# Two-layer trunk on one core: other reading orders behind five kinds of head groups, and a later start for the scaling of x's first block

## The chip, the cores and the metric

The kernel runs on 1 core of one Trainium2 chip. The metric is device time in microseconds (us) of one launch. Before the change it is 1683.47 us, the median of 3 runs (1681.31 to 1684.75).

## What is computed

With DEPTH = 1 only the attention layer runs: an RMSNorm, one wide projection into q, k, v and a gate, stick-breaking attention in 32 heads, the SiLU gate, an output projection, the residual and a last RMSNorm. x is 256 rows of 4096, all in float32.

```
def attn_branch(xn, w_in, w_out):
    proj = xn @ w_in                       # (256 x 4096) @ (4096 x 16384)
    q, k, v, g = jnp.split(proj, 4, axis=-1)   # then 32 heads of 128
...
    z = q k^T * scale; log_fail = where(s < t, log_sigmoid(-z), 0)
    a = where(s < t, exp(log_sigmoid(z) + suffix_sum(log_fail)), 0);  o = a @ v
    return (o * jax.nn.silu(g)) @ w_out    # (256 x 4096) @ (4096 x 4096)
h = x + attn_branch(rms_norm(x, norm_attn), w_in, w_out);  return rms_norm(h, final_norm)
```

## The kernel before, in words

**The products.** Both projections are cut into units of 2 x 256 columns from each of two places of the weights (16 units, 0 to 15, for the first projection, 4 for the second), and each unit into 16 steps (0 to 15) over the inner dimension, 256 deep each. Unit 0 is multiplied plainly, 8 products a step; from unit 1 on, a Strassen-like scheme takes 7 products in some steps (`SEVEN`) and 8 in the others. A step's weights come in two tiles, which are cut into parts; parts are numbered n through the whole program, and in unit 0 step s has parts 2s and 2s+1. A float32 product is made of three float32r matmuls (`mm3`): with x = sh + sl and w = wh + wl, a "high" and a "low" half each, TensorE adds up sh\*wh, sh\*wl and sl\*wh in one bank of PSUM. In each of the three the half of x is the stationary operand (128 x 128) and the half of w is the moving one (128 x 512). ScalarE (ACT) makes the highs by casting, VectorE (DVE) the lows by subtraction.

**The order of reading.** The 512 moving columns and the 512 columns of the result are not gone through from left to right. `RUNS` gives two orders: "e" goes through them in runs of 8 (as 4 x 16 x 8) and "c" in runs of 4 (as 4 x 32 x 4); the result is the same. A word of three letters gives the orders of a product's three matmuls. Most products have the word "eee"; the first of each step has "ecc" (`IN_STEP`).

**The heads' groups.** The heads of unit u are worked on while the products of unit u+1 run. For each of a unit's two heads (i = 0, 1) TensorE is given four small groups of other matmuls between two products: `turn` (four transposes of q and k), `scores` (q times k), `scan` (the suffix sums, and a transpose of the gate) and `values` (weights times v, and a transpose). They go in ahead of all waiting products. The function `ten` records such a group, and sets the words of the next seven products: `BEHIND_OTHERS`, which is ("ccc", "ecc", "eee", "eee", "eee", "eee", "ecc"). Where the next group comes sooner than seven products, it sets the list anew. A table `BEHIND`, empty before, could put other words at the head of the list for a group by its name.

**What sets the order of the work.** The class `Plan` is a planner that runs while the program is built: each piece of work has an engine, a cost in ns and a key (its due time), and each engine's next instruction is the waiting one with the smallest key at the planned time. The chip then works through each engine's list strictly in that order; a wait that the planner did not foresee holds up all that stands behind it on the engine.

**The first steps.** `blocks_of(0)` takes x's first block. DVE makes its high and low half at once. The tail of it, reached when these are recorded, is for unit 1: ACT scales the block by the norm's gain in place (`scaled`, two instructions on 128 x 256, written xs<-xs,gcol), and `sums_of` then takes a difference on DVE (128 x 256) and its halves (sh on ACT, sl on DVE, 128 x 256 each). Its key is that of step 2 (`BLOCKS_LATER`), but the work is free to go as soon as an engine has nothing more urgent that is ready. Later blocks of x (xs1, xs2, ...) are loaded by SyncE (SP), scaled and cast on ACT and summed on DVE (four 128 x 128). Their unit 0 halves carry the names sh and sl with the block's number: sl4 is the low half for step 4.

Of the kernel before, what the change touches and what calls it, by code (L numbers as in the profile page):

```python
# [19 lines left out]
P = 128  # L20
# [7 lines left out]
NB = D // CW  # L28
# [6 lines left out]
RUNS = {"e": (4, 8), "c": (4, 4), "g": (2, 8)}  # L35
BEHIND_OTHERS = ("ccc", "ecc", "eee", "eee", "eee", "eee", "ecc")
IN_STEP = ("ecc", "ecc")
BEHIND = {}
WARM, WARM_SHORT, IDLE = 10, 5, 640


# [70 lines left out]
def tensor_ns(n):  # L112
    return 0.4167 * n + 8.5 if n > 128 else 109.0
# [138 lines left out]
def kernel(  # L252
# [10 lines left out]
    nc = Plan(tc)  # L263
# [14 lines left out]
    def minus(out_, full, part):  # L278
        nc.vector.tensor_tensor(out=out_, in0=full, in1=part.bitcast(F32), op=ALU.subtract)
# [49 lines left out]
    def soon(c=4.0):  # L329
        return nc.here + 1e3 * c  # L330
# [13 lines left out]
    FULL_P, FULL_S = (P,) * 2, (W,) * 2  # L344

    since_others, words = 0, BEHIND_OTHERS

    def ten(emit, *n, what):
        def others():
            nonlocal since_others, words  # L350
            first_ = BEHIND.get(what, ())
            since_others, words = 0, first_ + BEHIND_OTHERS[len(first_) :]
            emit()

        return nc.work("tensor", 40 + sum(tensor_ns(m) for m in n), others, nc.here - 1e4, wait=400)
# [209 lines left out]
    def blocks_of(i):  # L565

        key = place_of[0, i]
        tag = ("one", "two", "s", "s")[i % 4]
        yield nc.take(tag)
        pool, inside, bufs = (wp, "s", SINGLES) if tag == "s" else (ap, tag, 1)  # L570
        y = pool.tile([P, KT, S], F32, tag=inside, name=f"xs{i}", bufs=bufs)
        y4 = y.rearrange("p k (a b) -> p (k a) b", a=NT)
        h, l = new_forms(i, "s")
        gain = lambda c: gcol[:, i * KT + c : i * KT + c + 1]
        if i:
            yield moved(
                "sync", lambda: nc.sync.dma_start(y, xT[i]), [KT * S], key - 1, hold=True, wait=1300 * i - 600 if i < 4 else 0
            )

            def scaled():  # L580
                for c in range(KT):
                    nc.scalar.activation(y[:, c, :], y[:, c, :], AF.Copy, scale=gain(c))
                nc.scalar.copy(h[:, 0:4, :], y4)

            yield act(scaled, (S, S, 2 * S), key - 2e3)
            yield dve(lambda: minus(l[:, 0:4, :], y4, h[:, 0:4, :]), 2 * S, key)
        else:
            yield moved("scalar", lambda: nc.scalar.dma_start(gcol, gain_in), [KC], key - 1)
            yield moved("scalar", lambda: nc.scalar.dma_start(y, xT[i]), [KT * S], key - 1, hold=True)
            for c in range(KT):  # L590
                hc, lc = (t[:, 2 * c : 2 * c + 2, :].rearrange("p a b -> p (a b)") for t in (h, l))

                yield dve(
                    lambda: nc.vector.tensor_scalar(out=hc, in0=y[:, c, :], scalar1=gain(c), scalar2=None, op0=ALU.mult),
                    S, key - 1,
                )
                nc.tell(("sh", c))
                yield nc.until(("low", 0, c))
                yield dve(
                    lambda: nc.vector.scalar_tensor_tensor(  # L600
                        out=lc, in0=y[:, c, :], scalar=gain(c), in1=hc.bitcast(F32), op0=ALU.mult, op1=ALU.subtract
                    ),
                    S, key - 1,
                )
        nc.tell(("form", "s", i))
        later = place_at(0, i + BLOCKS_LATER)
        if not i:

            def scaled():
                for c in range(KT):  # L610
                    nc.scalar.activation(y[:, c, :], y[:, c, :], AF.Copy, scale=gain(c))

            yield act(scaled, (S, S), later)
        yield from sums_of(i, y4, "n", later)
        nc.give(tag)
# [214 lines left out]
    BW = 3 * P  # L830
    not_before = off.broadcast_to([P, 2, P])

    def head(u, i):
        act_ = lambda *w: act(*w, soon(4.0 if u else HEADS_FIRST))
        yield nc.take("att", "gh", sooner=True)
        tr = att.tile([P, 2, S], F32, tag="att", name=f"tr{u}_{i}")

        def turn():
            for k in range(2):
                for t in range(NT):  # L840
                    c = k * CW + i * P
                    nc.tensor.transpose(tr[:, k, t * P : (t + 1) * P], st["qk", u][:, t, c : c + P], ident)

        yield ten(turn, P, P, P, P, what=("turn", i))
        if i == HG - 1:
            nc.give("one")
        qk = wp.tile([P, 2, S], F32, tag="gh", name=f"qkT{u}_{i}", bufs=ROWS)
        yield act_(lambda: nc.scalar.copy(qk, tr), 2 * S)
        nc.give("att")
        yield nc.take("att", sooner=True)  # L850
        bank = att.tile([P, W], F32, tag="att", name=f"z{u}_{i}")
        z, gT = bank[:, 0:BW], bank[:, BW:W]

        def turned(to, t):
            nc.tensor.transpose(to, st["gv", u][:, t, i * P : (i + 1) * P], ident)

        def scores():
            kw = dict(stop=False, skip_group_check=True)
            nc.tensor.matmul(z[:, 0:P], qk[:, 1, P:S], qk[:, 0, P:S], start=True, **kw)
            nc.tensor.matmul(z[:, P:BW], qk[:, 1, 0:P], qk[:, 0, :], start=False, **kw)  # L860
            diagonal = z[:, 0 : 2 * P].rearrange("p (a b) -> p a b", a=2)
            nc.tensor.matmul(diagonal, ident_b, not_before, start=False, **kw)

        yield ten(scores, *FULL_P, *FULL_S, 2 * P, what=("scores", i))
        nc.give("gh")
        yield nc.take("gh", sooner=True)

        f = wp.tile([P, BW], F32, tag="gh", name=f"f{u}_{i}", bufs=ROWS)

        def soft():  # L870
            nc.scalar.activation(f, z, AF.Softplus, scale=scale)
            nc.scalar.activation(f, f, AF.Copy, scale=1.0 / scale)

        yield act_(soft, (BW + TABLE, BW))
        yield nc.take("gh", "gh", sooner=True)
        fh, fl = (wp.tile([P, BW], F32R, tag="gh", name=f"f{k}{u}_{i}", bufs=ROWS) for k in "hl")
        yield act_(lambda: nc.scalar.copy(fh, f), BW)
        yield dve(lambda: minus(fl, f, fh), BW)
        nc.give("gh")

        if i == 0:
            yield nc.until(("gate", u))

        def scan():
            kw = dict(start=False, skip_group_check=True)
            nc.tensor.matmul(z, neg_tri, fh, stop=False, **kw)
            nc.tensor.matmul(z, neg_tri, fl, stop=False, **kw)
            nc.tensor.matmul(z[:, 2 * P : BW], neg_one, fh[:, 0:P], stop=False, **kw)
            nc.tensor.matmul(z[:, 2 * P : BW], neg_one, fl[:, 0:P], stop=True, **kw)
            turned(gT, 0)  # L890

        yield ten(scan, BW, BW, P, P, P, what=("scan", i))
        nc.give("gh", "gh")
        gated = st["gv", u][:, :, i * P : (i + 1) * P]
        yield nc.take("gh", sooner=True)
        a = wp.tile([P, BW], F32, tag="gh", name=f"a{u}_{i}", bufs=ROWS)


        def weights_of():
            nc.scalar.activation(a, z, AF.Relu, scale=-scale)  # L900
            nc.scalar.activation(a, a, AF.Exp, scale=-1.0)

        yield act_(weights_of, (BW, BW + TABLE))
        yield act_(lambda: nc.scalar.copy(gated[:, 0, :], gT), P)
        nc.give("att")
        yield nc.take("att", sooner=True)
        bank2 = att.tile([P, BW], F32, tag="att", name=f"o{u}_{i}")
        o, gT2 = bank2[:, 0:S], bank2[:, S:BW]
        v = lambda t: st["gv", u][:, t, CW + i * P : CW + (i + 1) * P]

        def out_of_head():
            kw = dict(skip_group_check=True)
            nc.tensor.matmul(o, v(0), a[:, P:BW], start=True, stop=False, **kw)
            nc.tensor.matmul(o[:, P:S], v(1), a[:, 0:P], start=False, stop=True, **kw)
            turned(gT2, 1)

        yield ten(out_of_head, *FULL_P, *FULL_S, P, what=("values", i))
        nc.give("gh")
        yield act_(lambda: nc.scalar.copy(gated[:, 1, :], gT2), P)
        o2 = o.rearrange("p (t b) -> p t b", t=NT)  # L920
        yield dve(lambda: nc.vector.tensor_tensor(out=gated, in0=o2, in1=gated, op=ALU.mult), S)
        nc.give("att")
# [444 lines left out]
```

## Time and profile before

| | |
|---|---|
| three runs | 1681.31, 1683.47, 1684.75 us |
| the profiled execution | 1683.75 us, span 1681.7 us |
| TensorE (PE) busy | 1666.9 us (99%), 7736 matmuls |
| weight loads (PEld) | 1410.1 us (84%) |
| VectorE (DVE) busy | 1611.1 us (96%) |
| ScalarE (ACT) busy | 1265.1 us (75%) |
| granted TensorE clock | 0.997 over the span |

The span goes from the first to the last instruction; 2.05 us of the profiled execution lie outside it. Matmuls are pipelined: each is shown as busy for about 0.38 us, but the next one starts 0.22 us after it. So what counts in a timeline is the distance from one start to the next, called the pitch here. In a profile's rows acc is a product's bank, tr, z and o are tiles of the heads' groups, wh and wl a part's halves, sh and sl the halves of x. All of TensorE's instructions have one source line, that of a helper, so rows are found by names and times.

### The profile page before, as it was taken

Reading aid. Unit: us, or ns where it says so; the run is one execution under the profiler, and the core shown is the slowest. Engines: PE = TensorE matmul, PEld = TensorE weight load, DVE = VectorE, ACT = ScalarE, POOL = GpSimd, SP = SyncE. Lnnn points to the kernel's source line nnn. Section 1 sums busy time; section 2 is a strip of 40 time slices with the busy share of each in tenths; the row PEclk is TensorE's granted clock in tenths of the full one; section 3 lists DMA queues with packets and bytes.
Section 4 is the critical chain, followed back from the end, with each engine's and each line's share of the span. In section 5 each row is a group of like instructions: output and inputs, shape, how many; then the busy total and the mean of one; then the engine's idle time right before and its main releaser. Section 6 shows DMA issues by size and latency. Waiting matters only on the chain.

```text
span 1681.7 us, 25051 instructions
## 1 busy us (share of the span) xinstructions
PE 1666.9 (99%) x7736; PEld 1410.1 (84%) x7736; DVE 1611.1 (96%) x1851; ACT 1265.1 (75%) x1665; POOL 366.0 (22%) x448
## 2 busy tenths in 40 slices
PE   9999999999999999999999999999999999999997
PEld 7888888888888888888888888888888888888885
DVE  9899999999999999999999999999999978999997
ACT  8896868686868696968686868686878766665664
POOL 0022222222222222222222221222222112212110
PEclk9999999999999999999999999999999999999998
DMA  9978898989897989797989897979898978888895
GB/s 340 350 187 255 228 253 226 263 221 261 225 265 212 271 209 279 199 282 200 278 204 279 216 265 214 260 225 255 229 249 233 290 252 251 268 251 269 254 313 189
DMA packets 254325, 419.31 MB, mean 249 GB/s; under 512 B 28912, under 2 KB 77296, under 8 KB 254192
## 3 DMA queue, kind: packets, MB, share of 16 engines
q1 hardware_dynamic: 195696, 356.34, 63.8%
q0 software_dynamic: 58208, 61.11, 21.8%
q8 instruction: 60, 0.98, 0.3%
q14 instruction: 73, 0.60, 0.1%
q10 hardware_dynamic: 288, 0.28, 0.1%
HBM read 408.17 MB, written 9.44 MB: 248 GB/s over the span
## 4 chain that ended last, share of the span: by engine, by line
PE 98%; DVE 1%; DMA 0%; ACT 0%; issue 0%; SPq 0%; DVEq 0%; ACTq 0%
PE acc L135 93%; PE z L135 3%; PE o L135 1%; PE tr L135 1%; DMA raw<-in_w_in_dram 0%; DVE wl L135 0%; DVE h L135 0%; ACT xs L135 0%; DVE xs L135 0%; SPq L135 0%; ACT sq L135 0%; ACT wh L135 0%; DVE wh L135 0%; DVE scalars L135 0%; ACT scalars L135 0%
## 5 line engine op out<-in xcount | busy, mean ns | idle before, releaser
L135 ACT CAST wh<-raw 128x1024 fp32r<-128x1024 f32 (+1 forms) x1019 | 935.8, 965 | 315.4 <-PE acc L135 131.3
L135 DVE TENSOR_TENSOR wl<-raw,wh 128x1024 fp32r<-128x1024 f32 (+1 forms) x830 | 991.6, 1221 | 35.5 <-PE acc L135 12.7
L135 PE MATMUL acc<-wh,sh 128*128 128x512 f32 x2048 | 767.1, 388 | 0.0
L135 PE MATMUL acc<-wh,sl 128*128 128x512 f32 x1883 | 721.7, 383 | 0.0
L135 PE MATMUL acc<-wl,sh 128*128 128x512 f32 x1718 | 655.1, 381 | 1.1 <-DVE wl L135 1.1
L135 POOL DMA_DIRECT2D raw<-in_w_in_dram x330 | 284.0, 942 | 1000.9 <-DMA raw<-in_w_in_dram 333.0
L135 PEld LDWEIGHTS acc<-wh,sh 128*128 128x128 f32 x2048 | 384.7, 188 | 67.9 <-ACT sh L135 0.5
L135 PEld LDWEIGHTS acc<-wh,sl 128*128 128x128 f32 x1883 | 353.1, 188 | 64.4 <-DVE sl L135 0.4
L135 PEld LDWEIGHTS acc<-wl,sh 128*128 128x128 f32 x1718 | 322.5, 188 | 57.8 <-DVE wl L135 1.9
L135 DVE TENSOR_TENSOR raw<-raw 128x512 f32<-128x512 f32 x378 | 361.0, 955 | 4.3 <-DMA raw<-in_w_in_dram 1.2
L135 PE MATMUL acc<-wh,oh 128*128 128x512 f32 x512 | 193.0, 384 | 0.2
L135 PE MATMUL acc<-wh,ol 128*128 128x512 f32 x488 | 186.9, 383 | 0.0
L135 PE MATMUL acc<-wl,oh 128*128 128x512 f32 x464 | 177.2, 382 | 0.0
L135 DVE TENSOR_TENSOR wh<-raw,wh 128x512 fp32r<-128x512 f32 x189 | 130.0, 688 | 1.7 <-ACT wh L135 1.7
L135 PEld LDWEIGHTS acc<-wh,oh 128*128 128x128 f32 x512 | 96.0, 187 | 18.7 <-DVE h L135 0.9
L135 PEld LDWEIGHTS acc<-wh,ol 128*128 128x128 f32 x488 | 91.5, 187 | 16.4
L135 ACT ACT_TABLE_LOAD x81 | 103.9, 1283 | 1.4
L135 PEld LDWEIGHTS acc<-wl,oh 128*128 128x128 f32 x464 | 87.0, 187 | 16.3 <-DVE wl L135 0.7
L135 POOL DMA_DIRECT2D raw<-in_w_out_dram x48 | 41.7, 967 | 172.8 <-DVE wl L135 49.6
L135 POOL DMA_DIRECT2D p<-spill x28 | 17.7, 654 | 88.0 <-DVE ol L135 50.7
L135 DVE SCALAR_TENSOR_TENSOR gv_sb<-acc,scalars,gv_sb 128x512 f32<-128x512 f32 x45 | 33.8, 750 | 0.0
L135 ACT CAST oh<-p 128x512 fp32r<-128x512 f32 (+3 forms) x47 | 21.3, 470 | 14.8 <-DVE p L135 12.7
(89 smaller groups left out, 713.4 us busy)
## 6 DMA issues: line engine op xcount, KB each, us to landing
raw<-in_w_in_dram SPq DMA_DIRECT2D x1024, 256.0 KB, 4.4
raw<-in_w_out_dram SPq DMA_DIRECT2D x256, 256.0 KB, 4.8
raw<-in_w_in_dram POOLq DMA_DIRECT2D x330, 128.0 KB, 5.0
p<-spill POOLq DMA_DIRECT2D x28, 256.0 KB, 4.3
raw<-in_w_out_dram POOLq DMA_DIRECT2D x48, 128.0 KB, 5.8
xr<-in_x_dram SPq DMA_DIRECT2D x16, 256.0 KB, 5.3
spill<-gv_sb POOLq DMA_DIRECT2D x32, 128.0 KB, 4.5
xres<-in_x_dram SPq DMA_DIRECT2D x16, 256.0 KB, 5.9
```

The costliest lines, as they stand in the source:

```text
L135: return self.tc.keep_in_program_order(getattr(self.engine, name)(*args, **kw))
```

## The change

It does two things. `BEHIND` now has whole lists of seven words for five of the eight groups of a unit (`scores`, `scan` and `values` of the first head, `turn` and `scan` of the second), used in units 2 to 14 alone; the other three groups, and all groups of units 0, 1 and 15, keep `BEHIND_OTHERS`. And the tail of `blocks_of(0)` is not begun before the first low half of part 2, which is the first part of step 1 (the second step), is recorded as done: `("low", 2, 0)`.

```
+BEHIND = {
+    ("scores", 0): ("cec", "eee", "eee", "eee", "eee", "eee", "ecc"),
+    ("scan", 0): ("ccc", "eee", "eee", "eee", "eee", "eee", "ecc"),
+    ("values", 0): ("cee", "eee", "eee", "eee", "eee", "eee", "ecc"),
+    ("turn", 1): ("eee", "ecc", "eee", "eee", "eee", "eee", "ecc"),
+    ("scan", 1): ("cee", "eee", "eee", "eee", "eee", "eee", "ecc"),
+}
...
-            first_ = BEHIND.get(what, ())
-            since_others, words = 0, first_ + BEHIND_OTHERS[len(first_) :]
+            u, *group = what
+            words = BEHIND.get(tuple(group), BEHIND_OTHERS) if 1 < u < NB - 1 else BEHIND_OTHERS
+            since_others = 0
...
         if not i:
+            yield nc.until(("low", 2, 0))
 
             def scaled():
```

The first edit leaves TensorE's list as it is but for the shape of some matmuls. In the rows below, of TensorE behind the `scores` of the first head of unit 3 (z is that group's tile, acc4 a bank of unit 4), the last number pair tells the order: 32x4 is "c", 16x8 is "e". Before:

```order
L135 MATMUL z3_0_3362<-off_143,ident_b_144 128x256
L135 MATMUL acc4_4_3357<-wh194_3239,sh0_80 128x4x32x4
L135 MATMUL acc4_4_3357<-wl194_3269,sh0_80 128x4x32x4
L135 MATMUL acc4_4_3357<-wh194_3239,sl0_81 128x4x32x4
L135 MATMUL acc4_5_3378<-wh195_3253,sh0_80 128x4x16x8
L135 MATMUL acc4_5_3378<-wl195_3285,sh0_80 128x4x32x4
L135 MATMUL acc4_5_3378<-wh195_3253,sl0_81 128x4x32x4
L135 MATMUL acc4_5_3378<-wh195_3253,sh0_80 128x4x16x8
```

After the change, the same place:

```order
L141 MATMUL z3_0_3362<-off_143,ident_b_144 128x256
L141 MATMUL acc4_4_3357<-wh194_3239,sh0_80 128x4x32x4
L141 MATMUL acc4_4_3357<-wl194_3269,sh0_80 128x4x16x8
L141 MATMUL acc4_4_3357<-wh194_3239,sl0_81 128x4x32x4
L141 MATMUL acc4_5_3378<-wh195_3253,sh0_80 128x4x16x8
L141 MATMUL acc4_5_3378<-wl195_3285,sh0_80 128x4x16x8
L141 MATMUL acc4_5_3378<-wh195_3253,sl0_81 128x4x16x8
L141 MATMUL acc4_5_3378<-wh195_3253,sh0_80 128x4x16x8
```

The second matmul went from "c" to "e", and so did the fifth and the sixth; nothing else moved.

The second edit moves instructions on ACT, DVE and SP within the first 16 steps. On DVE the difference of x's first block (xs0) goes from ahead of the low of part 2 to behind that of part 3, and ACT's two scalings of that block go from ahead of part 2's high to behind part 3's. Farther on, DVE's rows for steps 4 and 5 (names: wl10 and wl11 are the lows of parts 10 and 11, sl4 the low half of x for step 4) read before:

```order
L135 TENSOR_TENSOR xs3_91<-xs3_91 128x128 x4
L135 TENSOR_TENSOR wl10_359<-raw_76,wh10_342 128x1024
L135 TENSOR_TENSOR sl4_252<-xs4_250,sh4_251 128x512
L135 TENSOR_TENSOR sl2_90<-xs2_88,sh2_89 128x128
L135 TENSOR_TENSOR sl3_93<-xs3_91,sh3_92 128x384
L135 TENSOR_TENSOR wl11_385<-raw_76,wh11_368 128x1024
L135 TENSOR_TENSOR xs4_250<-xs4_250 128x128 x4
```

And after:

```order
L141 TENSOR_TENSOR xs3_91<-xs3_91 128x128 x4
L141 TENSOR_TENSOR sl2_90<-xs2_88,sh2_89 128x128
L141 TENSOR_TENSOR wl10_357<-raw_76,wh10_342 128x1024
L141 TENSOR_TENSOR wl11_378<-raw_76,wh11_361 128x1024
L141 TENSOR_TENSOR sl4_281<-xs4_279,sh4_280 128x512
L141 TENSOR_TENSOR sl3_93<-xs3_91,sh3_92 128x384
L141 TENSOR_TENSOR xs4_279<-xs4_279 128x128 x4
```

So sl4 now stands behind wl11 and a small sl2. The seven rows are the same pieces of work on both sides, and DVE's next rows, up to sl5 and the sums of x's block 5, are the same again. On SP the load of x's block 4 goes behind one tile of weights, and the loads of parts 12 and 15 go back by two places and that of part 14 by one, past loads of x.

More of the change, by code (lines that the diff above doesn't have):

```diff
@@ L37 @@
 IN_STEP = ("ecc", "ecc")
-BEHIND = {}
+BEHIND = {
[5 more added lines that the diff above has]
+}
 WARM, WARM_SHORT, IDLE = 10, 5, 640
@@ L842, in turn @@
                     nc.tensor.transpose(tr[:, k, t * P : (t + 1) * P], st["qk", u][:, t, c : c + P], ident)
-        yield ten(turn, P, P, P, P, what=("turn", i))
+        yield ten(turn, P, P, P, P, what=(u, "turn", i))
         if i == HG - 1:
@@ L862, in scores @@
             nc.tensor.matmul(diagonal, ident_b, not_before, start=False, **kw)
-        yield ten(scores, *FULL_P, *FULL_S, 2 * P, what=("scores", i))
+        yield ten(scores, *FULL_P, *FULL_S, 2 * P, what=(u, "scores", i))
         nc.give("gh")
@@ L890, in scan @@
             turned(gT, 0)
-        yield ten(scan, BW, BW, P, P, P, what=("scan", i))
+        yield ten(scan, BW, BW, P, P, P, what=(u, "scan", i))
         nc.give("gh", "gh")
@@ L915, in out_of_head @@
             turned(gT2, 1)
-        yield ten(out_of_head, *FULL_P, *FULL_S, P, what=("values", i))
+        yield ten(out_of_head, *FULL_P, *FULL_S, P, what=(u, "values", i))
         nc.give("gh")
```

## The prediction

> **What bounds the kernel now.** I read the page first, then what TensorE waits for, then the chain that ended last, and last the timelines of the places that the change touches.
>
> ```profile
> PE 1666.9 (99%) x7736; PEld 1410.1 (84%) x7736; DVE 1611.1 (96%) x1851; ACT 1265.1 (75%) x1665; POOL 366.0 (22%) x448
> PE 98%; DVE 1%; DMA 0%; ACT 0%; issue 0%; SPq 0%; DVEq 0%; ACTq 0%
> ```
>
> ```profile
> PE warm L135 <- DVE idle L135: 1.3, 1, 1.3
> PE acc L135 <- DVE wl L135: 1.1, 2, 0.7
> ```
>
> TensorE is the chain: 98% of the span. Its waits for others are 2.4 us in 1681.7, 1.3 of them at the very start, where nothing changes. So there are two ways to gain: fewer stalls in the first steps (second edit), and a shorter distance from one matmul's start to the next, the pitch (first edit). The pitch of undisturbed work is read from the chain, from the stretch behind a unit's last group:
>
> ```profile
> 378.08 47.67 PE acc L135 x216
> ...
> 461.07 47.67 PE acc L135 x216
> ...
> 1207.95 47.67 PE acc L135 x216
> ```
>
> That is 0.2207 us for one matmul, and the same 47.67 us for the same 216 stands in each unit's chain, 82.99 us apart, up to 1207.95. The timing repeats, so what one unit shows may be multiplied. The best single rows lie 0.22 apart.
>
> The pitch is not always that. Here is TensorE after it had waited at 34.0 us, in a run of matmuls that all read in the order "e":
>
> ```profile
> 34.77 0.49 PE L135 MATMUL acc<-wh,sl 128*128 128x512 f32 x1
> 35.10 0.38 PE L135 MATMUL acc<-wh,sh 128*128 128x512 f32 x1
> ...
> 39.93 0.39 PE L135 MATMUL acc<-wh,sh 128*128 128x512 f32 x1
> 40.16 0.39 PE L135 MATMUL acc<-wl,sh 128*128 128x512 f32 x1
> ```
>
> ```profile
> 35.09:40.17 5.08, 5.08 (x24) 1.00 0.91 319
> ```
>
> From 35.10 to 40.16 there are 22 steps: 0.230 us each, with no wait between them, and the last column but two says that the granted clock was 1.00. So there is a slow pitch, 0.010 us above the fast one, which is not the clock's, follows an interruption and holds on for 22 matmuls of order "e". The next "c" pair stands at 40.16 and 40.40; a few matmuls later the pitch is 0.22 again. This is what the words behind the groups are about: a group is an interruption too.
>
> **The five lists.** Behind each of the five groups, in unit 3's heads (matmuls of unit 4), with the first matmul behind the group and the tenth (for `values` the eleventh) after it:
>
> ```profile
> 345.73 0.47 PE L135 MATMUL acc<-wh,sh 128*128 128x512 f32 x1
> 346.05 0.39 PE L135 MATMUL acc<-wl,sh 128*128 128x512 f32 x1
> ...
> 347.17 0.39 PE L135 MATMUL acc<-wh,sh 128*128 128x512 f32 x1
> ...
> 347.87 0.38 PE L135 MATMUL acc<-wh,sh 128*128 128x512 f32 x1
> 348.09 0.38 PE L135 MATMUL acc<-wl,sh 128*128 128x512 f32 x1
> ```
>
> ```profile
> 352.41 0.47 PE L135 MATMUL acc<-wh,sh 128*128 128x512 f32 x1
> 352.72 0.38 PE L135 MATMUL acc<-wl,sh 128*128 128x512 f32 x1
> ...
> 354.73 0.38 PE L135 MATMUL acc<-wl,sh 128*128 128x512 f32 x1
> ...
> 359.16 0.47 PE L135 MATMUL acc<-wh,sh 128*128 128x512 f32 x1
> ...
> 361.69 0.39 PE L135 MATMUL acc<-wh,sl 128*128 128x512 f32 x1
> ...
> 362.27 0.47 PE L135 MATMUL acc<-wh,sh 128*128 128x512 f32 x1
> ...
> 364.61 0.38 PE L135 MATMUL acc<-wl,sh 128*128 128x512 f32 x1
> ...
> 371.75 0.47 PE L135 MATMUL acc<-wh,sh 128*128 128x512 f32 x1
> 372.06 0.38 PE L135 MATMUL acc<-wl,sh 128*128 128x512 f32 x1
> ...
> 374.08 0.38 PE L135 MATMUL acc<-wl,sh 128*128 128x512 f32 x1
> ```
>
> Ten steps at 0.22 are 2.20, eleven 2.42. The excess is 0.16 for `scores` of the first head (2.36), 0.12 for its `scan` (2.32), 0.11 for its `values` (2.53), 0.14 for `turn` of the second head (2.34) and 0.13 for its `scan` (2.33): 0.66 us in a unit. Some of it no order can touch: the first step is 0.31 or 0.32 (345.73 to 346.05, 352.41 to 352.72, 371.75 to 372.06), 0.09 over the pitch, because the second matmul's weights come in behind the group. Five times 0.09 is 0.45, so 0.21 us in a unit is left for the words. Units 2 to 14 are 13, so the whole prize is 0.21 x 13 = 2.7 us, and it can't be more behind these groups.
>
> How much of it do the new lists take? In the old list the order changes three times in the first three products (ccc, ecc, eee). In the new ones it changes once behind both `scan` and behind `values`, twice behind `turn`, three times (cec) behind `scores`. The clean cases (`scan` and `values` of the first head, no slow rows) have 0.02 to 0.03 above the first step for three changes; one change instead would leave a third. Behind `scores` three steps of order "e" in a row (347.17 to 347.87) take 0.70, the slow pitch; with "cec" I can't tell whether it comes. No row has the new lists, so the term is bounded: at best all of the 2.7 us, at worst the loss worked out under the rivals. I take half, a choice: it is what the three groups with a single change would give (two thirds of 0.03, 0.02 and 0.04), and some of the 0.07 and 0.05 behind the other two. **Term: -1.4 us.** It is on the path in full, since TensorE waits for nobody there.
>
> **The later scaling.** What it is aimed at is TensorE's first stall, at 11.75:
>
> ```profile
> 9.07 0.90 ACT L135 ACTIVATE xs<-xs,gcol 128x256 f32<-128x256 f32 x2
> 9.19 0.69 DVE L135 TENSOR_TENSOR sl<-xs,sh 128x512 fp32r<-128x512 f32 x1 [0.21 <-ACT sh L135]
> 10.00 1.61 DVE L135 TENSOR_TENSOR xs<-xs 128x256 f32<-128x256 f32 x5
> 11.53 1.22 DVE L135 TENSOR_TENSOR wl<-raw,wh 128x1024 fp32r<-128x1024 f32 x1
> 11.75 0.39 PE L135 MATMUL acc<-wh,sh 128*128 128x512 f32 x1
> 12.80 0.50 PE L135 MATMUL acc<-wl,sh 128*128 128x512 f32 x1 [0.67 <-DVE wl L135]
> 14.83 1.27 DVE L135 TENSOR_TENSOR xs<-xs 128x128 f32<-128x128 f32 x4
> ```
>
> TensorE starts a matmul at 11.75 and the next at 12.80, 0.83 late, waiting for the low of part 2 (11.53 to 12.75). Ahead of it DVE does five sums; one, the 128 x 256 of x's first block, goes away. Five take 1.61 and four 1.27, so the low starts 0.34 earlier, and so does TensorE. ACT, 0.90 of scaling lighter, has part 2's high ready before DVE wants it.
>
> That gain doesn't last. DVE has work without a pause from here to 41.60:
>
> ```profile
> 26.22 1.22 DVE L135 TENSOR_TENSOR wl<-raw,wh 128x1024 fp32r<-128x1024 f32 x1
> 27.36 1.35 DVE L135 TENSOR_TENSOR sl<-xs,sh 128x512 fp32r<-128x512 f32 x3
> 29.00 0.38 PE L135 MATMUL acc<-wh,sl 128*128 128x512 f32 x1
> 32.75 1.22 DVE L135 TENSOR_TENSOR wl<-raw,wh 128x1024 fp32r<-128x1024 f32 x1
> 34.02 0.69 DVE L135 TENSOR_TENSOR sl<-xs,sh 128x512 fp32r<-128x512 f32 x1
> 41.60 0.90 DVE L135 TENSOR_TENSOR sl<-xs,sh 128x512 fp32r<-128x512 f32 x2 [1.37 <-ACT sh L135]
> ```
>
> TensorE's second stall ends with sl5, DVE's row at 34.02: the matmul at 34.77 is its first use. In both programs the same pieces of DVE's work stand ahead of sl5, only in another order, and DVE's idle time up to there is the 0.21 at 9.19. So sl5 can't be ready more than 0.21 earlier, and TensorE, however early it arrives, goes on at 34.77 as before. The 0.34 turns into waiting. It even waits at a new place: sl4 goes behind one more low (1.14, from 26.22 to 27.36) and a small sl2, so it starts near 28.7 and ends near 29.35, while TensorE, 0.34 earlier, wants it at 28.66. That wait of some 0.7 makes the stall at 34.0 shorter by as much. The moved loads on SP have room: part 12's low is at 32.75, and its first matmul at 39.93. **Term: 0.** Its bounds: -0.21 by DVE's idle time and -0.22 if the slow pitch behind the stall (22 x 0.010) doesn't come, so -0.4; on the other side a new idle spot on DVE while it waits for ACT, up to the largest of the first 42 us, 1.37, since ACT's order changed too.
>
> **Sum.** 1683.75 (the profiled execution, span 1681.7 and 2.05 around it) - 1.4 + 0 = 1682.35. That execution is 0.28 above the median 1683.47, so against the median it is 1682.1.
>
> **The rivals.** First, the orders do nothing for the sum: the words may decide only where the excess is paid. For it: the excess behind five groups of different kinds differs by 0.05 only. Against it: 0.230 against 0.22 in the rows above with the same clock. Time: the median, 1683.5. [...]
>
> Second, on the other side: the slow pitch stays. The new lists have fewer "c"s in the products right behind a group, and 35.10 to 40.16 shows what "e" alone does after an interruption. If TensorE stays slow from the second product on until the next "c" (the seventh list, or the next group), that is 15 matmuls behind `scores` and each `scan` (three groups), 9 behind `values` and 3 behind `turn`: 57 x 0.010 = 0.57 us in a unit in place of the 0.21 there now, so +0.36 x 13 = +4.7 us, 1688.2. It decides from where the slow stretches cost more than what they replace: 0.21 / 0.010 = 21 matmuls in a unit, four a group; over 0.2% worse (3.4 us, about what a measurement of this kernel can tell from no change) needs 0.26 more, 47 in all.
>
> Third, more than the prize: the groups whose lists stay (`turn` of the first head, `scores` and `values` of the second) may be entered in a better state, and the first steps may gain their 0.4. If the other three drop as the five at best, by 0.04 each, that is 1.6 us more: 1683.5 - 2.7 - 1.6 - 0.4 = 1678.8.
>
> That the lists are not in the program is ruled out by the rows of its order.
>
> **How the numbers follow.** Small gain as forecast 0.54 (1680.8 to 1683.2), nothing 0.25 (1683 to 1684.5), slow pitch 0.11 (1685 to 1689), large gain 0.10 (1678.5 to 1680.1). The likeliest gives 1682.1. The range leaves out half of the large gain and most of the slow case: 1679.8 to 1685.2; it takes in both bounds of the first steps and half the spread of the runs. Faster by over 0.2% (below 1680.1): the large gain and a little of the forecast, 0.13. Slower by over 0.2% (above 1686.8): most of the slow case, 0.09. Within: 0.78.
>
> **What would show it.** In the profile after: behind the five groups, first to tenth later matmul, 2.27 to 2.33 us where it was 2.32 to 2.36; behind `scores` no three steps of 0.70. Unit to unit, 82.99 should become about 82.88. In the first steps the matmul at 12.80 comes at about 12.46, a wait for sl4 appears near 28.7, and the use of sl5 stays within 0.3 of 34.77. The prediction is wrong if a unit gets longer, if it loses more than 0.3 us, or if TensorE is over 0.5 us earlier or later at 45 us.

## The result, and the profile after

The kernel after the change takes 1687.78 us, the median of 9 runs (1685.98 to 1689.26), beside 1683.47 before (9 runs); the ratio is 1.0029, with a 95% interval of 1.0021 to 1.0038. It is slower, by 4.3 us.

The page of the kernel after, busy times, and what TensorE's matmuls waited for:

```profile
PE 1669.5 (99%) x7736; PEld 1411.0 (84%) x7736; DVE 1611.8 (96%) x1851; ACT 1264.7 (75%) x1665; POOL 366.0 (22%) x448
```

```profile
PE acc L141 <- DVE wl L141: 0.8, 2, 0.4
```

TensorE is 98% of the chain as before, and its matmuls do not wait longer (the line shown, and the 1.3 us at the start as before); the 7736 matmuls themselves take more time. The chain of waits shows where. Its pieces (start, length, what, how many matmuls) behind the units' last groups, before, where the prediction doesn't show them:

```profile
130.41 46.34 PE acc L135 x210
295.10 47.67 PE acc L135 x216
...
1290.93 49.63 PE acc L135 x225
```

And after:

```profile
130.83 46.34 PE acc L141 x210
212.52 47.67 PE acc L141 x216
295.54 47.66 PE acc L141 x216
378.89 47.66 PE acc L141 x216
...
1295.78 49.63 PE acc L141 x225
```

At 130 us the two already differ by 0.4, which comes from the first steps. The long stretch of 216 has kept its length. The period from one to the next was 82.99; after, the first one with the new lists (unit 2's heads) has 83.02, and each of the next twelve 83.35. From 295 to the row of 225 it is 995.83 before and 1000.24 after: +4.41, which is the whole of the loss. (The two profiled executions differ by only 2.1 in their spans, because the last projection of the one after, a single piece of 1179 matmuls in 259.94, had none of the short stalls that it has before (weight loads that wait 0.46, 0.54 and 0.45 us at 1512.26, 1590.91 and 1592.59), nor the slow pitch behind them (from 1512.59 to 1516.05 15 steps of 0.231); this run was the fastest of its nine, and the kernel with only the list behind the second `scan`, below, has the same single piece, 259.79.)

One unit's heads in detail, by the pieces between the groups. The seven rows stand behind `turn`, `scores`, `scan`, `values` of the first head and `turn`, `scores`, `scan` of the second. Before, unit 3:

```profile
343.20 2.01 PE acc L135 x9
345.98 6.01 PE acc L135 x27
352.66 5.98 PE acc L135 x27
359.40 2.68 PE acc L135 x12
362.52 2.69 PE acc L135 x12
365.97 5.36 PE acc L135 x24
371.99 5.33 PE acc L135 x24
```

After, unit 2 (two of its seven rows) and unit 3:

```profile
263.40 5.98 PE acc L141 x27
...
289.27 5.51 PE acc L141 x24
```

```profile
343.64 2.06 PE acc L141 x9
346.46 6.22 PE acc L141 x27
353.33 6.03 PE acc L141 x27
360.12 2.65 PE acc L141 x12
363.21 2.66 PE acc L141 x12
366.63 5.34 PE acc L141 x24
372.62 5.51 PE acc L141 x24
```

In unit 2 the rows are as long as before or a little shorter, but for the last one, behind the second head's `scan`: 5.51 where it was 5.33. From unit 3 on, the first three rows are longer too, `scores` most: 6.22 for 27 matmuls is 0.230 for one, the slow pitch. Unit 2 has the same lists and needs 5.98 there. So the list behind `scores` seems to be good or bad by what stands ahead of it, and what is new ahead of it is the last unit's second `scan`, with `values`, the stretch of 216 and `turn` in between. TensorE behind such a `scan`, rows from the start and the end of its list of 21 matmuls:

```profile
372.69 0.38 PE L141 MATMUL acc<-wl,sh 128*128 128x512 f32 x1
372.91 0.39 PE L141 MATMUL acc<-wh,sl 128*128 128x512 f32 x1
...
377.07 0.40 PE L141 MATMUL acc<-wh,sl 128*128 128x512 f32 x1
377.31 0.39 PE L141 MATMUL acc<-wh,sh 128*128 128x512 f32 x1
377.53 0.38 PE L141 MATMUL acc<-wl,sh 128*128 128x512 f32 x1
```

The step into 372.91 is 0.22. From there to 377.31, behind the list's last word with its "c" pair, are 19 steps in 4.40 us, 0.232 each; then it is 0.22 again. No gap and no wait lies in it, and the granted clock was 1.00:

```profile
372.86:377.13 4.27, 4.27 (x20) 1.00 0.95 254
```

### The profile page after: what moved, and what is told of

It reads as the page before. It is cut to its first block, busy times and chain, and to the rows that moved or that the text cites. A ratio compares the mean times of both kernels' runs of the same rounds, so it can differ in the third digit from the quotient of the medians.

```text
span 1683.8 us, 25052 instructions
## 1 busy us (share of the span) xinstructions
PE 1669.5 (99%) x7736; PEld 1411.0 (84%) x7736; DVE 1611.8 (96%) x1851; ACT 1264.7 (75%) x1665; POOL 366.0 (22%) x448
## 4 chain that ended last, share of the span: by engine, by line
PE 98%; DVE 1%; DMA 0%; ACT 0%; issue 0%; SPq 0%; DVEq 0%; ACTq 0%
PE acc L141 93%; PE z L141 3%; PE o L141 1%; PE tr L141 1%; DMA raw<-in_w_in_dram 0%; DVE wl L141 0%; DVE h L141 0%; SPq L141 0%; DVE xs L141 0%; ACT xs L141 0%; ACT sq L141 0%; DVE sl L141 0%; ACT wh L141 0%; ACT sh L141 0%; DVE wh L141 0%
```

## The experiments

Two theories stood against each other. One: the slow pitch is a state that TensorE enters behind some groups, that lasts through matmuls of order "e", that a change of the order ends, and that is handed from one group to the next, so that lists can't be priced one by one. The other: each list has a price of its own, whatever stands ahead of it. Differences of the lists are read from the period between the chain's long pieces, which repeats to 0.01 us in most units, since whole times spread by some 3 us.

**One edit at a time.** First the later scaling without the lists:

```
-BEHIND = { ... five lists ... }
+BEHIND = {}
```

> The later scaling alone, with the empty table of before. If the lists are the whole loss, a unit's period stays 82.99 us and the time is that of before, 1683.5, within 1 us. If the later scaling is part of the loss, the time is 1.5 us or more above before with the period unchanged.

Ratio 0.9997 (0.9988 to 1.0007), period 82.99. Then the lists without the later scaling:

```
-            yield nc.until(("low", 2, 0))
```

> The five lists alone, with the scaling as before. If the lists are the whole loss, the period of units 3 to 14 is 83.35 us as in the changed kernel and the time is 4 to 4.5 us above before. If the loss needs both edits (another start leading to another state at unit 3), the period is at or below 82.99.

Ratio 1.0025 (1.0016 to 1.0035), period 83.35 as in the kernel after. The lists are the whole loss.

**Which list.** Both edits, without the list behind the second head's `scan`:

```
-    ("scan", 1): ("cee", "eee", "eee", "eee", "eee", "eee", "ecc"),
```

> Both edits, without the list behind the second head's scan. If that list both costs 0.18 us itself and spoils the state in which the next unit's first turn is entered, all units behave as unit 2 of the changed kernel does ahead of it: period 82.99 - 0.03 - 0.03 - 0.03 - 0.03 - 0.03 = 82.84, and 1.9 us less than before. If the bad state at the first turn comes from the other lists, the slow stretch behind the first head's scores stays: period 82.99 + 0.05 + 0.21 + 0.04 - 0.09 = 83.20, 2.7 us more than before.

```profile
295.00 47.67 PE acc L140 x216
377.84 47.67 PE acc L140 x216
```

The period is 82.84, and the ratio 0.9984 (0.9974 to 0.9993): faster than both kernels. The other four lists gain 0.15 us in a unit.

Not every unit of the profiled execution, the slowest of its ten (1683.29; the median is 1680.48), is like that: four of its 13 periods are 83.16 to 83.35. In the first of them a weight load of the first `scores` waits for ACT, and the stretch behind that group is long:

```profile
842.16 0.52 PEld L140 LDWEIGHTS z<-qkT 128*128 128x128 f32 x4 [0.42 <-ACT qkT L140]
```

```profile
843.19 6.15 PE acc L140 x27
```

In the next unit, without such a wait, it is 6.22. The other two periods have waits of the same kind (the group takes 1.03 and 0.85 us in place of 0.77), and 5.99 and 6.21 behind them. So a short hold-up of TensorE can lead into the slow pitch as well, with the good lists and without the fifth.

Then that list alone, the other four removed:

```
-    ("scores", 0): ("cec", "eee", "eee", "eee", "eee", "eee", "ecc"),
-    ("scan", 0): ("ccc", "eee", "eee", "eee", "eee", "eee", "ecc"),
-    ("values", 0): ("cee", "eee", "eee", "eee", "eee", "eee", "ecc"),
-    ("turn", 1): ("eee", "ecc", "eee", "eee", "eee", "eee", "ecc"),
```

> Both edits, with the list behind the second head's scan alone. If that list is enough for the bad state, its own stretch is 0.18 us longer and from unit 3 on the first turn is 0.05 longer (2.50 for 2.45 us), with the first step behind it near 0.316 for 0.306: period about 83.20. If it only costs itself, 83.17 and a first turn of 2.45.

```profile
378.62 47.66 PE acc L137 x216
461.82 47.66 PE acc L137 x216
```

The period is 83.20, 0.21 over before; one run, 1683.49. If prices were each list's own, all five would cost 0.21 - 0.15 = 0.06 over before; they cost 0.37. The 0.3 between is what the list behind `scan` makes of the lists behind the next unit's first `scores` and `scan`. In this kernel, with the old list there, that stretch stays good:

```profile
343.53 2.06 PE acc L137 x9
346.35 5.99 PE acc L137 x27
```

The turn's stretch has the 2.06 of the kernel after, so the group seems to be entered in the same state; only with the new list ("cec", then "eee") does the slow pitch follow.

**Does a change of the order end it?** All five lists, but one "c" pair of the bad list also in the third product, not only in the seventh:

```
-    ("scan", 1): ("cee", "eee", "eee", "eee", "eee", "eee", "ecc"),
+    ("scan", 1): ("cee", "eee", "ecc", "eee", "eee", "eee", "ecc"),
```

> The changed kernel, but the third list behind the second head's scan is ecc for eee. If a c pair ends the slow pitch, the slow stretch there ends within 4 to 8 matmuls of the third product in place of at the seventh: the group's stretch is 6.02 to 6.08 us for 6.165 (5.986 with the old list). If the length of the slow stretch has another cause, it stays at 6.16.

```profile
343.19 2.01 PE acc L141 x9
345.96 5.98 PE acc L141 x27
...
371.82 5.40 PE acc L141 x24
```

The stretch is 5.40 in place of 5.51, and the next unit's first two are good again, 2.01 and 5.98, with every list behind them the same as in the kernel after. The period is 82.91, the time of one run 1682.51. (The expectation counts the group's own 0.65 us too: 6.05 in place of 6.165.) The pair (373.27 and 373.50) ended the slow pitch where it was put: from 372.12 to 373.97 are eight steps of 0.231, from there to 376.17 ten of 0.220. What the next unit lost goes with it. A pair does not do so everywhere: behind the first `scores` of the kernel after, the list's closing pair starts at 350.67 and 350.90, and the six steps from 351.13 to 352.52, up to the next group, still take 0.232 each.

**Lists without any "c".** All eight groups get seven words "eee" in units 2 to 14:

```
+BEHIND = {(g, i): ("eee",) * 7 for g in ("turn", "scores", "scan", "values") for i in range(HG)}
```

> Both edits, with seven times eee behind all eight groups of units 2 to 14; the pair of order c in the first product of each step stays. If the slow pitch lasts until the next c, each group that ends in the slow state is followed by 0.230 us a matmul up to the next step's pair (up to 24 matmuls, 0.24 us a group): period between 83.2 and 84.5 us. If the slow pitch ends by itself after a few matmuls, the period is under 82.9, since there are fewer changes of order than in any other list.

The period is 83.51 (546.92 to 630.43 in the chain), the time of one run 1690.9. In these units `scores` of the first and of the second head have 6.20 and 5.52, slow nearly throughout, but the two `scan`s 6.02 and 5.36. Behind the first `scan` of unit 5:

```profile
521.13 0.39 PE L135 MATMUL acc<-wl,sh 128*128 128x512 f32 x1
...
522.52 0.38 PE L135 MATMUL acc<-wl,sh 128*128 128x512 f32 x1
...
523.40 0.38 PE L135 MATMUL acc<-wh,sl 128*128 128x512 f32 x1
```

From 521.13 to 522.52 are six steps of 0.232, from there to 523.40 four of 0.22. All of them are of order "e", so here the slow pitch ended without a "c". The same, and the first product of a step plain too:

```
-IN_STEP = ("ecc", "ecc")
+IN_STEP = ("eee", "eee")
```

> Both edits, seven times eee behind all groups of units 2 to 14, and eee in the first product of each step everywhere. If nothing but an order c (or a new interruption) ends the slow pitch, whole stretches of 216 matmuls run at 0.230 us (49.8 us for 47.67) wherever they are entered slow, and the last projection, with no groups, too: 1700 us or more. If it ends by itself, or the c orders are not what ends it, the time is 1686 or less.

```profile
1421.49 104.46 PE acc L135 x474
1525.97 162.90 PE acc L135 x705
```

One run, 1703.0, period 83.77. These two pieces are the last projection, where no group stands. The first has 0.2204 for a matmul. Then a weight load waits 0.44 us for DVE, and behind it the pitch is 0.2311 to the end, for 705 matmuls. The words are "eee" on both sides (but for the first seven products of the first piece), and the granted clock was 0.998 over the run: were it the cause, 163 of the 1701 us at 0.2204 / 0.2311 = 0.954 of full speed would alone leave 0.996. Nearly the whole of unit 0, behind its first stall, runs like that too (82.36 us for 356, 0.2313 each, at a granted clock of 1.00 from 13.4 to 94 us): with no "c" at all the slow pitch did not end by itself in either place. Not all "e" is slow, though: the stretch of 216 has 47.60 in most units, less than the 47.67 before. In one it has 49.87, behind a `values` group that took 0.90 us in place of 0.76. So "e" after "e" can be had at 0.22 too, and what decides is how the stretch is entered.

**The same list at other places.** The four good lists, and behind `scores`, `scan` and `values` of the second head the list that serves its `turn`:

```
-    ("scan", 1): ("cee", "eee", "eee", "eee", "eee", "eee", "ecc"),
+    ("scores", 1): ("eee", "ecc", "eee", "eee", "eee", "eee", "ecc"),
+    ("scan", 1): ("eee", "ecc", "eee", "eee", "eee", "eee", "ecc"),
+    ("values", 1): ("eee", "ecc", "eee", "eee", "eee", "eee", "ecc"),
```

> The changed kernel, with the list that serves the second head's turn (eee, ecc, then eee) behind its scores, scan and values too. The four lists that gain keep their period of 82.84 us if the first turn is still entered in the good state. The new three: if a list is good or bad by itself, each gains 0.02 to 0.03 as behind turn, period 82.76, 3.0 us less than before. If it is good or bad by the state in which it is met, at least one of the three leaves a slow stretch (0.05 to 0.2 us longer than the old list), and a list behind values may spoil the first turn.

```profile
365.75 5.32 PE acc L143 x24
371.72 5.43 PE acc L143 x24
377.91 47.77 PE acc L143 x216
```

Behind `scores` it gains 0.02 (5.34 in the kernel after), behind `scan` and `values` it loses 0.10 each (5.33 and 47.67 before). The period is 83.02 and the ratio 1.0002 (0.9993 to 1.0012). With its good place alone:

```
+    ("scores", 1): ("eee", "ecc", "eee", "eee", "eee", "eee", "ecc"),
```

> The four lists that gain (without the one behind the second head's scan), and eee, ecc, then eee behind the second head's scores. By the state theory that stretch is 6.081 us as in the run with more lists (6.102 with the old list), and the old list behind scan still brings the unit to the same state, so the period is 82.82 us and the time 2.2 us less than before. If the scan is now met in another state, its stretch is not 5.986 and the period 82.9 or more.

```profile
294.85 47.67 PE acc L141 x216
377.67 47.67 PE acc L141 x216
```

The period is 82.82, the ratio 0.9986 (0.9976 to 0.9995). It and the kernel without the list behind the second `scan` are both faster than before, and the intervals don't tell them apart.

**Another way to change the entry.** The four good lists, and no "c" pair in the first product of a step in units 2 to 15:

```
-        elif p["i"] == 0 and k == 0:
+        elif p["i"] == 0 and k == 0 and not 1 < p["u"] < NB:
```

> The four lists that gain, and eee for ecc in the first product of each step of units 2 to 15. In the state that is fast, a pair of order c costs 0.013 us in two of three steps (rows 0.230 and 0.225 behind it) and nothing in the third. If the unit stays fast by its lists alone, the stretch behind values of the second head is 0.08 us shorter (48.35), the period 82.7, and the time 3.5 to 4 us less than before. If a group leaves the slow pitch behind and the pairs were what ended it, stretches of 24 to 216 matmuls run at 0.230: period above 83.

```profile
343.29 2.04 PE acc L140 x9
346.09 6.22 PE acc L140 x27
...
378.36 47.57 PE acc L140 x216
```

The stretch of 216 gains the 0.10 that its pairs cost, but the next unit's `turn` is entered otherwise (2.04 in place of 2.01), and behind `scores` the good list gives 6.22, to the digit what the kernel after has. The next period is 83.03, the ratio 1.0002 (0.9993 to 1.0012). The loss lies behind the first `scores` and `scan`; the stretch of 216 stays fast. This is the slow stretch behind the first `scores` without any new list behind the second `scan`: the list there is one way to such an entry, not the only one.

**Reading from left to right.** Both orders set to one run of 512, and no lists:

```
-RUNS = {"e": (4, 8), "c": (4, 4), "g": (2, 8)}
+RUNS = {"e": (1, 512), "c": (1, 512), "g": (2, 8)}
```

> The later scaling, and all products read from left to right, with no runs and no changes of order. If the slow pitch is a matter of the orders e and c, matmuls 0.216 to 0.222 us apart everywhere and a time of 1690 or less. If left to right is worse than either, and the runs of 8 were chosen against it, the pitch is 0.224 us or more in undisturbed stretches, and the time over 1700.

```profile
301.76 49.01 PE acc L135 x216
```

One run, 1723.86, period 85.12. The pitch is 49.01 / 216 = 0.2269, between the fast one (0.2207) and the slow (0.231).

## Why the prediction was wrong

It forecast 1682.1, no change to speak of; the time lies outside its range, on the side of its second rival.

**The bound** was named rightly: TensorE's pitch is the time, and in the kernels before and after it waits for nobody behind the five groups. So is the slow pitch, 0.230 at a granted clock of 1.00.

**The lists, -1.4.** This step failed, in the sign. It counted the changes of order in each list and gave each change a price, so that fewer changes were a gain, and it took each group by itself. A unit got longer, the prediction's own first sign of being wrong. For four of the five the size was about right: they gain 0.15 us in a unit, 0.15 x 13 = 1.9 us over 13 units. The fifth was judged by its kin: "cee" behind `values` of the first head leaves the pitch fast (2.65 after, 2.68 before), and the same word behind the second head's `scan` leaves it slow for 19 matmuls. And the step had no term for what one group hands to the next, which is the larger part: of the 83.35 - 82.84 = 0.51 us that the fifth list costs beside the other four, 0.18 lie behind its own group (5.51 - 5.33) and the rest in the next unit's first three stretches (6.22 - 5.98 behind `scores` alone is 0.24).

**The prize of 2.7 us** was worked out as the most that words behind these groups could give. No kernel here goes past it; the best, which also has a list behind a sixth group, gains 82.99 - 82.82 = 0.17 us in a unit, 2.2 us.

**The second rival** was what happened: 0.36 us in a unit and 1688.2, where 0.37 and 1687.78 were measured. Its places were partly others. It had slow stretches behind all five groups, 57 matmuls; the runs show them behind the second `scan` and the next unit's first `scores` above all, 0.51 / 0.010 = some 51 matmuls, with `values` and the second head's `turn` clean. That the two sums lie so close is in part luck: it priced groups that stayed fast, and had nothing for what is handed on. It was given 0.11, less than its own rows say for it: 22 steps of "e" at 0.230, and fast again soon behind a "c" pair. The excess over the first step, from which the -1.4 was taken, could not show a list that wasn't there.

**The later scaling, 0**, was right, and for the reason given: DVE has no slack (before, its gaps from 6 us to sl5 are 0.21 us at 9.19 and 0.12 at 10.00). Without the lists, TensorE's second matmul of part 2 and its first use of sl4:

```profile
12.63 0.49 PE L135 MATMUL acc<-wl,sh 128*128 128x512 f32 x1
...
29.44 0.49 PE L135 MATMUL acc<-wh,sl 128*128 128x512 f32 x1 [0.24 <-DVE sl L135]
```

The first goes from 12.80 to 12.63 (12.46 forecast), and the wait for sl4 is there as named: DVE begins it at 28.70 (28.7 forecast), and its matmul starts at 29.44 (29.35 forecast for the end of sl4). DVE's row for sl5 stands at 34.03, where it was 34.02; the matmul that uses it starts at 35.05 (34.77 before, within the 0.3), and the stall at 34 is gone, in its place the slow pitch behind the wait for sl4 (33.21 to 35.97: twelve steps of 0.230). The chain's piece of 210 starts 0.06 earlier than before, at 130.35. In the profile of the kernel after the same rows stand some 0.5 later, at 13.11 and 29.92, and the use of sl5 at 35.55, outside the 0.3. Its weights were late: ACT's cast of part 1 starts at 7.38, after waiting 1.44 for its load; in the profile before it waits 0.70 and starts at 6.65. The piece of 210 starts at 130.67 in the kernel with the lists alone, where nothing of the first steps is changed, and at 130.28 to 130.61 in the others whose first steps are those of the kernel after. So its 0.4 is of the size by which executions differ, and not shown to be the edit's.

**The first rival**, that the orders do nothing, fell: the lists, which change nothing else, moved the time by 4 us. The pitch itself differs by the order of reading and the entry: the chains here have 0.2207 us (before) and 0.2313 (no "c", unit 0), both at a granted clock of 1.00, and 0.2269 read from left to right, where it was 0.998 over the run.

**What stays open.** The runs show that there are two ways to be behind a group, that a "c" pair behind it can end the slow one, and that it carries over groups. Why a pair ends it in one place and not in another, and why it sometimes ends without one, was not settled, nor what in the chip holds this state, nor why some words after some groups lead into it; no trace shows the inside of a matmul.

## What to carry to other kernels

Where a row of the trace shows a slow mode at an unchanged clock, look first for what ends it, here often a pair of matmuls in another order of reading, and count how many instructions a change leaves without it. Price a repeated edit over two periods in a row, since the first (83.02) and the second (83.35) differ where a state is handed on. Edits to a list that hands on a state are tried one at a time: four of these five were a gain, and only the run without the fifth showed it.

## What the runs showed of the hardware

- Three pitches for the same matmul of 128 x 512: 0.2207 us (before) and 0.2313 (no "c"), both at a granted clock of 1.00, and 0.2269 (left to right, 0.998 over the run). The slow one can last: 705 matmuls in a row at 0.2311, behind a wait of 0.44 us.
- The "c" pair that can end it is nearly free: without its pairs the stretch of 216 has 47.57 instead of 47.67.
- Left to right, the plainest order, is the slowest of the kernels tried, by 2.13 us in a unit over before (85.12 to 82.99). Runs of 4 and 8 are faster here than one run of 512.
